# A router's top sixteen taken of two rows in turn, in finer steps between the low parts of streamed weights, and transposes in another ring of PSUM banks

## The chip, the cores and the metric

The kernel runs on one core of one Trainium2 chip. The metric is the device time in microseconds of one execution; the figure to compare is the median of three runs. The program's engines appear in the profile as PE (TensorE matmul) with PEld (its weight loads), DVE (VectorE), ACT (ScalarE), POOL (GpSimd) and SP (SyncE, which issues the DMAs). L12 is line 12 of the kernel.

## What is computed

The reference runs two layers of a first block (a pooling mixer or chunked attention, each followed by a convolutional feed-forward) and one layer of a second block (retention and stick-breaking attention, mixed by gates, followed by a layer of 16384 small experts) on one sequence of 256 positions of width 1024. The change lies in the experts' layer:

```python
def block(xb):
    q = (xb @ w_q).reshape(B, T, PEER_HEADS, 2, PEER_DKEY // 2).astype(jnp.float32)
    s1 = jnp.einsum('bthd,nd->bthn', q[..., 0, :], k1)
    s2 = jnp.einsum('bthd,nd->bthn', q[..., 1, :], k2)
    v1, i1 = lax.top_k(s1, PEER_TOPK)
    v2, i2 = lax.top_k(s2, PEER_TOPK)
    cand_s = (v1[..., :, None] + v2[..., None, :]).reshape(...)
    cand_i = (i1[..., :, None] * N_KEYS + i2[..., None, :]).reshape(...)
    top_s, pos = lax.top_k(cand_s, PEER_TOPK)
    idx = jnp.take_along_axis(cand_i, pos, axis=-1)
    g = jax.nn.softmax(top_s, axis=-1)
    u_sel = jnp.take(u_tab, idx, axis=0)
    h = jnp.einsum('bthkd,btd->bthk', u_sel, xb)
    a = (jax.nn.gelu(h.astype(jnp.float32)) * g).astype(xb.dtype)
    return jnp.einsum('bthk,bthkd->btd', a, jnp.take(v_tab, idx, axis=0))
```

There are 8 heads, 128 keys on either side and 16 kept of each (`PEER_TOPK`), so 128 x 128 experts.

## The kernel before

The kernel doesn't gather the chosen experts. It computes the products of x with all 16384 rows of `peer_u`, multiplies them by gates that are zero for experts not chosen, and multiplies by all rows of `peer_v`. The 256 positions are two blocks of 128. Every product in full precision is made of three matmuls (`mm3`, L107): weights and x are each split into a high part and a low part, the first two matmuls take the weights' high part (L109, L110) and the third their low part (L111).

The weights come from memory as a stream of slabs. For a slab, SP issues a DMA into one of three `raw` buffers, ACT rounds it to the high part `whi` (L72), and DVE (or POOL, for a counted few) subtracts to get the low part `wlo` (L80; L86 where the low parts are put off with `later=True` and given out by `lows`). Three high and three low buffers go round.

The experts' layer is `peer` (L747). PE, DVE and ACT there follow an order written out by hand: each engine runs its instructions in the order in which the program gives them out. Its parts, in time:

1. The query projections, 8 heads, 784.7 to 840.8 us (L777 to L803). For each head h a slab of `peer_wq`, 48 matmuls into the PSUM tile `qps`, and, one head later, `scores` (L968): a copy to SBUF on ACT (L972), 8 matmuls with the keys (`scps`, L976), a scaled copy into a `sc` buffer on ACT (L980). In heads 1 and 2 the normalized x of block 0 and 1 is also transposed (`transposed`, L206): 8 transposes into two PSUM tiles `pt`, read by ACT (L221) and DVE (L223) into `hn`, the x that all experts' products use.
2. The first loop over slabs of `peer_u` (L883), 128 experts and 24 matmuls each, numbered from 0. For slab i the program gives out the high part of slab i + 2 (ACT), some router work (DVE), the low part of slab i + 2 (DVE), and the 24 matmuls of slab i (`up`, PE, into `hps`); every second slab a gelu on ACT (L837). It ends when the router's work has all been given out.
3. The second loop (L905) over the slabs that are left. The 64 groups of four positions get their gates here: one-hot rows on DVE (L859, L862), 8 products on PE (L869, `gps`), and the result multiplied into h on DVE (L877) or copied on ACT (L879). `until` (L903) spreads the 64 groups evenly over the slabs that are left less three. The first products on PE stand behind the second slab of this loop.
4. The products with `peer_v` (L940), 1252 to 1602 us.

How much router work a slab gets is set by `side` (L751). The router is a generator, `route` (L983), that yields a price after each piece. `side(rout, upto)` runs pieces until the sum of the prices reaches `upto`; a yield of 0 (nothing to do yet, or a pause) ends the slab's share and lifts the sum to at least `upto - 1`. `upto` is 5 a head in the projections (L788) and 36 + 1.6 i for slab i (L885).

The router's pieces: for each of 8 heads, 2 blocks and 2 sides, `top16` of a row of 128 scores, price 1.2; then for each block the candidate sums (1.3), `top16` of 8 rows of 64 candidates at 0.9 each, the decoding of the codes `unstair` (L1060, 2.4), and for each side an equality (1.2), a product (1.2) and a tree of sums (L1033 to L1035, 1.4); a softmax with an exponential on ACT, two yields of 0, and three transposes with their copies (1.5). `top16` (L1083) is five VectorE operations: the 8 largest, their places, the row with these struck out, the 8 largest of that, their places. In the trace the searches for places and the striking out appear as two instructions each, a value load and the operation.

PSUM has 8 banks here: the ring "w" has three (`self.nw`), "acc" four, "o" one. In the projections "acc" is used by the score products alone. Of SBUF the router has two scratch rows for `top16` and five `sc` buffers for scores.

Of the kernel before, what the change touches and what calls it, by code (L numbers as in the profile page):

```python
# [8 lines left out]
F32 = mybir.dt.float32  # L9
# [5 lines left out]
OP = mybir.AluOpType  # L15
# [5 lines left out]
KT = D // 128  # L21
# [7 lines left out]
TOPK = 16  # L29
# [5 lines left out]
V_MIX0, V_FFN0, V_MIX1, V_FFN1, V_ATT2, V_FFN2 = 0, 8, 16, 24, 32, 40  # L35
# [11 lines left out]
class K:  # L47
# [155 lines left out]
            nc.scalar.activation(hi, src, AF.Copy, scale=g)  # L203
            nc.vector.scalar_tensor_tensor(lo, src, g, hi.bitcast(F32), op0=OP.mult, op1=OP.subtract)

    def transposed(self, hi, lo, src, b, kts, gcol=None, k0=0):  # L206

        nc = self.nc
        for k in range(0, kts, 4):
            n = min(4, kts - k)  # L210

            tag, bufs = ("o", 1) if kts == KT and b == 1 and k == 4 else ("w", self.nw)
            pt = self.ps.tile([128, 4, 128], F32, tag=tag, name="pt", bufs=bufs)
            for j in range(n):
                nc.tensor.transpose(pt[:, j, :], src[:, (k + j) * 128:(k + j + 1) * 128], self.ident)
            t = slice(b * 128, (b + 1) * 128)
            if gcol is None:
                self.split(hi[:, k0 + k:k0 + k + n, t], lo[:, k0 + k:k0 + k + n, t], pt[:, :n, :])
            else:
                for j in range(n):  # L220
                    nc.scalar.activation(hi[:, k0 + k + j, t], pt[:, j, :], AF.Copy, scale=self.gain(gcol + k + j))  # L221
                for j in range(n):
                    nc.vector.scalar_tensor_tensor(lo[:, k0 + k + j, t], pt[:, j, :], self.gain(gcol + k + j),  # L223
                                                   hi[:, k0 + k + j, t].bitcast(F32), op0=OP.mult, op1=OP.subtract)
# [522 lines left out]
    def peer(self, rt, wq_scope):  # L747
        tc, nc = self.tc, self.nc
# [17 lines left out]
        with ExitStack() as ctx:  # L766
# [6 lines left out]
            rout = self.route(rt["route"], pT, gp, iota)  # L773
            next(rout)
            prev, xn = None, []
            self.to_pool = 7
            for h in range(8):  # L777
                if h == 7:
                    wq = self.next()
                    self.wp = rt["slabs"]  # L780
                    self.nraw, self.nsplit, self.piece = 3, 3, 1024
                    self.start_stream(self.stream2())
                    self.prefetch(2)
                else:
                    self.prefetch(2)
                    wq = self.next()
                wh, wl = wq
                side(rout, h * 5.0)  # L788
                ps = self.ps.tile([128, 2, S], F32, tag="w", name="qps", bufs=self.nw)
                for m in range(2):  # L790
                    for k in range(KT):
                        c = slice(m * 1024 + k * 128, m * 1024 + (k + 1) * 128)
                        self.mm3(ps[:, m], wh[:, c], wl[:, c], self.hT[0][:, k], self.hT[1][:, k],
                                 k == 0, k == KT - 1)
                if prev:
                    self.scores(rt["route"], *prev)
                else:
                    self.r = self.factors()
                    hT = self.ring(rt["hn"], self.OFF)
                    xn = [self.normalized(b) for b in range(2)]  # L800
                if xn and h:
                    self.transposed(*hT, xn.pop(0), h - 1, KT, V_FFN2)
                prev = (h, ps)  # L803
            wq_scope.close()
            self.oh = pool("oh")
# [76 lines left out]
            last = None  # L882
            for i in range(N1):  # L883
                self.prefetch(3, later=True)
                if not side(rout, 36 + i * 1.6):  # L885
                    last = i
                    break
                self.lows()
                up(i)
                if i == 0:  # L890
                    self.scores(rt["route"], *prev)
                if i % 2:
                    gelu(i)
            else:
                last = N1
                for _ in rout:
                    pass
# [22 lines left out]
            acc = self.acc4()  # L920
            AH, AL = self.ring(rt["hn"], 0)
            a = {}
# [45 lines left out]
    def scores(self, rt, h, ps):  # L968

        nc = self.nc  # L970
        q = rt.tile([128, 2, S], F32, tag="pq", name="pq", bufs=2)
        nc.scalar.activation(q, ps, AF.Copy)  # L972
        sp = self.ps.tile([128, 2, 2, 128], F32, tag="acc", name="scps", bufs=4)
        for b in range(2):
            for s in range(2):
                nc.tensor.matmul(sp[:, b, s], q[:, s, b * 128:(b + 1) * 128], self.keys[:, s],  # L976
                                 start=True, stop=True)
        sc = rt.tile([128, 2, 2, 128], F32, tag="sc", name="scores", bufs=5)
        for b in range(2):
            nc.scalar.activation(sc[:, b], sp[:, b], AF.Copy, scale=self.r[b])  # L980
        self.sc.append(sc)

    def route(self, rt, pT, gp, iota):  # L983
# [8 lines left out]
        for h in range(8):  # L992
            while len(self.sc) <= h:
                yield 0
            for b in range(2):
                for s in range(2):
                    self.top16(rt, v[:, b, 2 * h + s], ix[:, b, 2 * h + s], self.sc[h][:, b, s])
                    yield 1.2
        for b in range(2):
            ixf = rt.tile([128, 16, TOPK], F16, tag="ixf", name="ixf", bufs=1)  # L1000
            nc.vector.tensor_copy(ixf, ix[:, b])
# [8 lines left out]
                nc.vector.tensor_tensor(o, v1[:, :, a:a + na, None].to_broadcast([128, 8, na, nb]),  # L1010
                                        v2[:, :, None, 0:nb].to_broadcast([128, 8, na, nb]), op=OP.add)
            yield 1.3
            for h in range(8):
                self.top16(rt, top[:, h], code[:, 2, h], cand[:, h])
                yield 0.9
            abf = rt.tile([128, 2, 8 * TOPK, 2], F16, tag="abf", name="abf", bufs=1)
            self.unstair(rt, abf, code)
            yield 2.4
            sel = rt.tile([128, 3, 8, TOPK], F32, tag="sel", name="sel", bufs=1)
            tt = nc.vector.tensor_tensor  # L1020
            for s in range(2):
                eq = rt.tile([128, 8 * TOPK, TOPK], F16, tag="eq", name="eq", bufs=1)
                of = lambda ap: ap.to_broadcast([128, 8 * TOPK, TOPK // 2, 2])
                tt(eq.rearrange("p k (a b) -> p k a b", b=2),
                   of(iota[:, 0:TOPK].rearrange("p (a b) -> p a b", b=2)[:, None]), of(abf[:, s][:, :, None, :]),
                   op=OP.is_equal)
                yield 1.2
                src = ixf.rearrange("p (h s) a -> p h s a", s=2)[:, :, s]
                e = eq.rearrange("p (h k) a -> p h k a", h=8)
                tt(e, e, src[:, :, None, :].to_broadcast([128, 8, TOPK, TOPK]), op=OP.mult)  # L1030
                yield 1.2

                for n in (8, 4, 2):  # L1033
                    tt(eq[:, :, 0:n], eq[:, :, 0:n], eq[:, :, n:2 * n], op=OP.add)
                tt(sel[:, s].rearrange("p h k -> p (h k)"), eq[:, :, 0], eq[:, :, 1], op=OP.add)  # L1035
                yield 1.4
            g = sel[:, 2]
            nc.vector.tensor_tensor(g, top, top[:, :, 0:1].to_broadcast([128, 8, TOPK]), op=OP.subtract)
            nc.scalar.activation(g, g, AF.Exp)
# [20 lines left out]
    def unstair(self, rt, ab, code):  # L1060

        nc = self.nc
        ts, stt = nc.vector.tensor_scalar, nc.vector.scalar_tensor_tensor
        for n in range(2):
            ts(code[:, n], code[:, 2], 3 - n, None, op0=OP.logical_shift_right)
        c = rt.tile([128, 3, 8, TOPK], F32, tag="codef", name="codef", bufs=1)
        nc.vector.tensor_copy(c, code)
        a, m = c[:, 0], c[:, 1]
        ts(a, a, -1.0, 0.0, op0=OP.add, op1=OP.max)
        stt(a, m, -6.0, a, op0=OP.add, op1=OP.max)  # L1070
        stt(a, c[:, 2], -48.0, a, op0=OP.add, op1=OP.max)
        flat = lambda ap: ap.rearrange("p h k -> p (h k)")[:, :, None].to_broadcast([128, 8 * TOPK, 2])
        nc.vector.tensor_copy(ab[:, 0], flat(a))

        f = rt.tile([128, 8, TOPK], F32, tag="first", name="first", bufs=1)
        ts(f, a, 8.0, 8.0, op0=OP.mult, op1=OP.add)
        stt(f, a, 16.0, f, op0=OP.mult, op1=OP.min)
        ts(m, a, 4.0, 24.0, op0=OP.mult, op1=OP.add)
        nc.vector.tensor_tensor(f, f, m, op=OP.min)
        stt(f, a, 48.0, f, op0=OP.add, op1=OP.min)  # L1080
        nc.vector.tensor_tensor(ab[:, 1], flat(c[:, 2]), flat(f), op=OP.subtract)

    def top16(self, rt, v, ix, s):  # L1083
        nc = self.nc
        t = rt.tile([128, 128], F32, tag="topk", name="topk", bufs=2)[:, :s.shape[1]]
        nc.vector.max(out=v[:, 0:8], in_=s)
        nc.vector.max_index(out=ix[:, 0:8], in_max=v[:, 0:8], in_values=s)  # L1087
        nc.vector.match_replace(out=t, in_to_replace=v[:, 0:8], in_values=s, imm_value=-3.0e38)  # L1088
        nc.vector.max(out=v[:, 8:16], in_=t)
        nc.vector.max_index(out=ix[:, 8:16], in_max=v[:, 8:16], in_values=t)  # L1090

    def finish(self):
        for b in range(2):
# [158 lines left out]
```

## Time and profile before

| | us |
|---|---|
| median of three runs | 1604.07 (1604.07 to 1605.76) |
| the profiled execution | 1604.23 |
| its span, first to last instruction | 1602.5 |
| PE busy / DVE busy / ACT busy / POOL busy in the span | 1565.4 / 1160.3 / 843.0 / 105.0 |

The span holds 26447 instructions, 278.66 MB moved by DMA (174 GB/s in the mean), and a mean granted TensorE clock of 0.995. An instruction's time in a row is from its start to its end; instructions of one engine overlap by a part of that, so what one costs its engine is read from one start to the next. Matmul ends are modelled.

### The profile page before, as it was taken

What the parts mean: (1) busy time and instruction counts of PE and PEld (TensorE: products, weight loads), DVE (VectorE), ACT (ScalarE), POOL (GpSimd) and SP (SyncE); (2) the same over time, 40 slices, a digit from 0 to 9 for tenths busy, and PEclk for the clock granted to TensorE, in tenths of its full rate; (3) what the DMA queues carried; (4) which work ended last, traced back from release to release, by engine and by line L of the source; (5) the groups of instructions that cost most, each with busy time, mean ns of one, the idle gap of its engine ahead of it and who ended that gap; (6) DMA issues with size and microseconds to landing.
All of it is one profiled execution on the core that took longest, in us unless ns stands there. A gap on an engine that the chain in (4) does not pass through costs nothing.

```text
span 1602.5 us, 26447 instructions
## 1 busy us (share of the span) xinstructions
PE 1565.4 (98%) x10190; PEld 1401.5 (87%) x10190; DVE 1160.3 (72%) x2479; ACT 843.0 (53%) x1563; POOL 105.0 (7%) x111
## 2 busy tenths in 40 slices
PE   5999999999999999999999999999999999999999
PEld 4999987779999887888898999999999888888887
DVE  7676777767767877675599987788888655555554
ACT  6555565565555647444554555454444544454453
POOL 5000020010000202000260000000000000000000
PEclk9999999999999999999999999999999999999999
DMA  5555464325555552455424555555555666666664
GB/s 218 181 196 198 168 237 175 132 83 192 201 183 201 187 183 106 152 178 200 167 76 136 167 174 169 170 171 159 170 161 170 186 197 196 189 194 196 194 192 152
DMA packets 58446, 278.66 MB, mean 174 GB/s; under 512 B 6480, under 2 KB 7376, under 8 KB 41680
## 3 DMA queue, kind: packets, MB, share of 16 engines
q1 hardware_dynamic: 58320, 276.97, 52.6%
q8 instruction: 80, 1.31, 0.3%
q14 instruction: 46, 0.38, 0.1%
HBM read 275.90 MB, written 1.05 MB: 173 GB/s over the span
## 4 chain that ended last, share of the span: by engine, by line
PE 87%; DVE 9%; issue 2%; ACT 1%; DMA 1%; POOL 0%; SPq 0%; DVEq 0%; ACTq 0%; POOLq 0%
PE acc L110 15%; PE acc L111 15%; PE acc L109 15%; PE hps L109 6%; PE hps L111 6%; PE hps L110 6%; PE up L110 5%; PE up L111 5%; PE up L109 5%; PE gps L869 2%; DVE wlo L86 1%; DVE wlo L80 1%; DVE topk L1088 1%; DVE ix L1087 1%; DVE ix L1090 1%
## 5 line engine op out<-in xcount | busy, mean ns | idle before, releaser
L72 ACT ACTIVATE whi<-raw 128x512 fp32r<-128x512 f32 (+1 forms) x764 | 556.3, 769 | 381.3 <-PE acc L111 158.4
L80 DVE TENSOR_TENSOR wlo<-raw,whi 128x512 fp32r<-128x512 f32 (+1 forms) x572 | 448.6, 812 | 137.7 <-ACT whi L72 137.5
L111 PE MATMUL hps<-hn,wlo 128*128 128x256 f32 x1024 | 289.2, 282 | 8.6 <-DVE wlo L86 8.5
L109 PE MATMUL hps<-hn,whi 128*128 128x256 f32 x1024 | 293.5, 287 | 0.0
L110 PE MATMUL hps<-hn,whi 128*128 128x256 f32 x1024 | 287.1, 280 | 0.0
L111 PEld LDWEIGHTS hps<-hn,wlo 128*128 128x128 f32 x1024 | 194.0, 189 | 10.7 <-DVE wlo L86 10.6
L110 PE MATMUL up<-hT,whi 128*128 128x256 f32 x704 | 197.8, 281 | 1.5 <-DVE hT L223 1.5
L109 PE MATMUL up<-hT,whi 128*128 128x256 f32 x704 | 198.1, 281 | 0.4 <-DVE hT L223 0.4
L111 PE MATMUL up<-hT,wlo 128*128 128x256 f32 x704 | 197.4, 280 | 0.0
L110 PE MATMUL acc<-wlo,hn 128*128 128x512 f32 x504 | 196.2, 389 | 0.0
L111 PE MATMUL acc<-whi,hn 128*128 128x512 f32 x504 | 196.2, 389 | 0.0
L109 PE MATMUL acc<-whi,hn 128*128 128x512 f32 x504 | 196.2, 389 | 0.0
L110 PEld LDWEIGHTS hps<-hn,whi 128*128 128x128 f32 x1024 | 194.5, 190 | 0.0
L109 PEld LDWEIGHTS hps<-hn,whi 128*128 128x128 f32 x1024 | 194.3, 190 | 0.0
L86 DVE TENSOR_TENSOR wlo<-raw,whi 128x1024 fp32r<-128x1024 f32 x128 | 155.8, 1219 | 14.8 <-ACT whi L72 14.1
L110 PEld LDWEIGHTS up<-hT,whi 128*128 128x128 f32 x704 | 133.6, 190 | 3.3 <-DVE hT L223 2.0
L109 PEld LDWEIGHTS up<-hT,whi 128*128 128x128 f32 x704 | 133.5, 190 | 2.1 <-issue 0.7
L111 PEld LDWEIGHTS up<-hT,wlo 128*128 128x128 f32 x704 | 133.6, 190 | 0.0
L110 PE MATMUL acc<-wlo,hT 128*128 128x512 f32 (+1 forms) x320 | 125.0, 391 | 2.2 <-DVE wlo L80 1.2
L80 POOL TENSOR_TENSOR wlo<-raw,whi 128x512 fp32r<-128x512 f32 x64 | 84.3, 1347 | 636.0 <-ACT whi L72 629.3
L111 PE MATMUL acc<-whi,hT 128*128 128x512 f32 (+1 forms) x320 | 124.7, 390 | 0.0
L109 PE MATMUL acc<-whi,hT 128*128 128x512 f32 (+1 forms) x320 | 124.4, 390 | 0.0
(291 smaller groups left out, 2486.1 us busy)
## 6 DMA issues: line engine op xcount, KB each, us to landing
raw<-in_peer_u SPq DMA_DIRECT2D x128, 512.0 KB, 3.6
raw<-in_peer_v SPq DMA_DIRECT2D x128, 512.0 KB, 3.6
raw<-in_wup SPq DMA_DIRECT2D x44, 1024.0 KB, 4.9
raw<-in_win SPq DMA_DIRECT2D x26, 1024.0 KB, 4.8
raw<-in_wdn SPq DMA_DIRECT2D x22, 1024.0 KB, 4.8
raw<-in_wqkv SPq DMA_DIRECT2D x12, 1024.0 KB, 4.9
raw<-in_wo SPq DMA_DIRECT2D x8, 1024.0 KB, 4.8
raw<-in_peer_wq SPq DMA_DIRECT2D x8, 1024.0 KB, 4.8
```

The source lines that it names most:

```text
L72: i = nc.scalar.activation(hi[:, c:c + n], raw[:, c:c + n], AF.Copy)
L80: low(*args, op=OP.subtract)
L86: self.nc.vector.tensor_tensor(*self.low_parts.pop(0), op=OP.subtract)
L109: mm(ps, lh, rh, start=start, stop=False)
L110: mm(ps, lh, rl, start=False, stop=False)
L111: mm(ps, ll, rh, start=False, stop=stop)
L869: nc.tensor.matmul(ps[:, j], jh[:, j], gh[:, n, j], start=n == 0, stop=n == 1)
L1087: nc.vector.max_index(out=ix[:, 0:8], in_max=v[:, 0:8], in_values=s)
L1088: nc.vector.match_replace(out=t, in_to_replace=v[:, 0:8], in_values=s, imm_value=-3.0e38)
L1090: nc.vector.max_index(out=ix[:, 8:16], in_max=v[:, 8:16], in_values=t)
```

## The change

`top16` takes two rows and gives out each operation for both before the next one, with a price after the first two operations and one after the last three. `unstair` becomes a generator with three prices (1.0, 1.3, 1.4) in place of one of 2.4. A tree of sums is priced 1.9 instead of 1.4. A slab gets 1.5 instead of 1.6. The scratch rows of `top16` have 4 buffers instead of 2, the scores 4 instead of 5. The transposes of the experts' x go into the "acc" ring in place of "w" (and "o" for half of the second block). Apart from the order of the operations, what is computed is the same.

```diff
-    def transposed(self, hi, lo, src, b, kts, gcol=None, k0=0):
+    def transposed(self, hi, lo, src, b, kts, gcol=None, k0=0, bank=None):
...
-            tag, bufs = ("o", 1) if kts == KT and b == 1 and k == 4 else ("w", self.nw)
+            tag, bufs = bank or (("o", 1) if kts == KT and b == 1 and k == 4 else ("w", self.nw))
...
                 if xn and h:
-                    self.transposed(*hT, xn.pop(0), h - 1, KT, V_FFN2)
+                    self.transposed(*hT, xn.pop(0), h - 1, KT, V_FFN2, bank=("acc", 4))
...
-                if not side(rout, 36 + i * 1.6):
+                if not side(rout, 36 + i * 1.5):
...
-        sc = rt.tile([128, 2, 2, 128], F32, tag="sc", name="scores", bufs=5)
+        sc = rt.tile([128, 2, 2, 128], F32, tag="sc", name="scores", bufs=4)
...
             for b in range(2):
-                for s in range(2):
-                    self.top16(rt, v[:, b, 2 * h + s], ix[:, b, 2 * h + s], self.sc[h][:, b, s])
-                    yield 1.2
+                yield from self.top16(rt, 1.2, [(v[:, b, 2 * h + s], ix[:, b, 2 * h + s], self.sc[h][:, b, s])
+                                                for s in range(2)])
...
-            for h in range(8):
-                self.top16(rt, top[:, h], code[:, 2, h], cand[:, h])
-                yield 0.9
+            for h in range(0, 8, 2):
+                yield from self.top16(rt, 0.9, [(top[:, i], code[:, 2, i], cand[:, i]) for i in (h, h + 1)])
             abf = rt.tile([128, 2, 8 * TOPK, 2], F16, tag="abf", name="abf", bufs=1)
-            self.unstair(rt, abf, code)
-            yield 2.4
+            yield from self.unstair(rt, abf, code)
...
-                yield 1.4
+                yield 1.9
...
         ts(a, a, -1.0, 0.0, op0=OP.add, op1=OP.max)
+        yield 1.0
         stt(a, m, -6.0, a, op0=OP.add, op1=OP.max)
         stt(a, c[:, 2], -48.0, a, op0=OP.add, op1=OP.max)
-        flat = lambda ap: ap.rearrange("p h k -> p (h k)")[:, :, None].to_broadcast([128, 8 * TOPK, 2])
         nc.vector.tensor_copy(ab[:, 0], flat(a))
 
         f = rt.tile([128, 8, TOPK], F32, tag="first", name="first", bufs=1)
         ts(f, a, 8.0, 8.0, op0=OP.mult, op1=OP.add)
+        ts(m, a, 4.0, 24.0, op0=OP.mult, op1=OP.add)
+        yield 1.3
         stt(f, a, 16.0, f, op0=OP.mult, op1=OP.min)
-        ts(m, a, 4.0, 24.0, op0=OP.mult, op1=OP.add)
         nc.vector.tensor_tensor(f, f, m, op=OP.min)
         stt(f, a, 48.0, f, op0=OP.add, op1=OP.min)
         nc.vector.tensor_tensor(ab[:, 1], flat(c[:, 2]), flat(f), op=OP.subtract)
-
-    def top16(self, rt, v, ix, s):
-        nc = self.nc
-        t = rt.tile([128, 128], F32, tag="topk", name="topk", bufs=2)[:, :s.shape[1]]
-        nc.vector.max(out=v[:, 0:8], in_=s)
-        nc.vector.max_index(out=ix[:, 0:8], in_max=v[:, 0:8], in_values=s)
-        nc.vector.match_replace(out=t, in_to_replace=v[:, 0:8], in_values=s, imm_value=-3.0e38)
-        nc.vector.max(out=v[:, 8:16], in_=t)
-        nc.vector.max_index(out=ix[:, 8:16], in_max=v[:, 8:16], in_values=t)
+        yield 1.4
+
+    def top16(self, rt, cost, rows):
+
+        vec = self.nc.vector
+        t = [rt.tile([128, 128], F32, tag="topk", name="topk", bufs=4)[:, :s.shape[1]] for _, _, s in rows]
+        for v, _, s in rows:
+            vec.max(out=v[:, 0:8], in_=s)
+        for v, ix, s in rows:
+            vec.max_index(out=ix[:, 0:8], in_max=v[:, 0:8], in_values=s)
+        yield cost
+        for (v, _, s), r in zip(rows, t):
+            vec.match_replace(out=r, in_to_replace=v[:, 0:8], in_values=s, imm_value=-3.0e38)
+        for (v, _, s), r in zip(rows, t):
+            vec.max(out=v[:, 8:16], in_=r)
+        for (v, ix, s), r in zip(rows, t):
+            vec.max_index(out=ix[:, 8:16], in_max=v[:, 8:16], in_values=r)
+        yield cost
```

## Rows read from the trace of the kernel before

**Rows 1.** Stretches: length, busy (instructions) of PE, PEld, DVE, ACT, POOL; PEclk, DMA.

```profile
840.80:952.50 111.70, 103.12 (x833) 101.00 (x832) 102.24 (x325) 55.41 (x68) 0.00 (x0) 0.97 0.51 157
952.50:1252.50 300.00, 300.00 (x2780) 296.91 (x2779) 249.87 (x485) 148.80 (x293) 0.00 (x0) 1.00 0.55 169
```

**Rows 2.** Waits of PE, 784.7 to 952.5: us in total, times, longest.

```profile
PE hps L111 <- DVE wlo L86: 8.5, 9, 2.6
```

**Rows 3.** PE in order of time: start, us, instruction, [idle before <-releaser].

```profile
800.94 0.39 PE L109 MATMUL qps<-hT,whi 128*128 128x256 f32 x1 [2.25 <-DVE hn L223]
...
849.78 0.38 PE L111 MATMUL hps<-hn,wlo 128*128 128x256 f32 x1 [1.98 <-DVE wlo L86]
...
886.26 0.39 PE L111 MATMUL hps<-hn,wlo 128*128 128x256 f32 x1 [1.25 <-DVE wlo L86]
...
928.20 0.39 PE L111 MATMUL hps<-hn,wlo 128*128 128x256 f32 x1 [2.62 <-DVE wlo L86]
```

**Rows 4.** Stretches as in rows 1: two behind long waits, three slabs without one.

```profile
850.73:854.14 3.41, 3.41 (x19) 3.41 (x18) 3.27 (x13) 0.23 (x1) 0.00 (x0) 0.50 0.62 168
929.24:932.65 3.41, 3.41 (x18) 3.41 (x17) 3.38 (x4) 0.00 (x0) 0.00 (x0) 0.50 0.75 259
935.26:943.74 8.48, 8.48 (x75) 8.48 (x74) 7.51 (x10) 5.25 (x6) 0.00 (x0) 1.00 0.69 207
```

**Rows 5.** DVE in order of time: one row of 128 and the next one's start.

```profile
801.83 0.29 DVE L1086 MAX8 v<-scores 128x8 f32<-128x128 f32 x1
802.15 0.09 DVE L1087 MATCH_VALUE_LOAD ix<-v,scores 128x8 f32 x1
802.23 0.28 DVE L1087 FIND_INDEX8 ix<-v,scores 128x8 uint32<-128x128 f32 x1
...
802.49 0.28 DVE L1088 MATCH_REPLACE8 topk<-v,scores 128x128 f32<-128x128 f32 x1
802.80 0.29 DVE L1089 MAX8 v<-topk 128x8 f32<-128x128 f32 x1
803.13 0.09 DVE L1090 MATCH_VALUE_LOAD ix<-v,topk 128x8 f32 x1
803.21 0.28 DVE L1090 FIND_INDEX8 ix<-v,topk 128x8 uint32<-128x128 f32 x1
803.41 0.28 DVE L1086 MAX8 v<-scores 128x8 f32<-128x128 f32 x1
```

**Rows 6.** DVE: a low part, the start of a row of 64, the next low part.

```profile
864.68 1.22 DVE L86 TENSOR_TENSOR wlo<-raw,whi 128x1024 fp32r<-128x1024 f32 x1
865.81 0.22 DVE L1086 MAX8 top<-cand 128x8 f32<-128x64 f32 x1
866.07 0.09 DVE L1087 MATCH_VALUE_LOAD code<-top,cand 128x8 f32 x1
...
867.06 1.21 DVE L86 TENSOR_TENSOR wlo<-raw,whi 128x1024 fp32r<-128x1024 f32 x1
```

**Rows 7.** DVE: decoding, first and last and the low part behind; a tree and what follows.

```profile
890.67 1.65 DVE L1034 TENSOR_TENSOR eq<-eq 128x1024 f16<-128x1024 f16 x3
...
892.82 1.23 DVE L1024 TENSOR_TENSOR eq<-iota,abf 128x2048 f16<-128x2048 f16 x1
...
923.30 0.36 DVE L1065 TENSOR_SCALAR code<-code 128x128 uint32<-128x128 uint32 x2
...
926.92 1.22 DVE L86 TENSOR_TENSOR wlo<-raw,whi 128x1024 fp32r<-128x1024 f32 x1
```

**Rows 8.** Start of the first loop: second head's first row, high parts, slab 2's products, low part.

```profile
811.72 0.28 DVE L1086 MAX8 v<-scores 128x8 f32<-128x128 f32 x1
...
835.34 2.00 ACT L72 ACTIVATE whi<-raw 128x1024 fp32r<-128x1024 f32 x2
...
847.41 0.28 PE L109 MATMUL hps<-hn,whi 128*128 128x256 f32 x1
...
848.52 1.21 DVE L86 TENSOR_TENSOR wlo<-raw,whi 128x1024 fp32r<-128x1024 f32 x1
```

More of the change, by code (lines that the diff above doesn't have):

```diff
@@ L1068, in unstair @@
         a, m = c[:, 0], c[:, 1]
+        flat = lambda ap: ap.rearrange("p h k -> p (h k)")[:, :, None].to_broadcast([128, 8 * TOPK, 2])
         ts(a, a, -1.0, 0.0, op0=OP.add, op1=OP.max)
+        yield 1.0
         stt(a, m, -6.0, a, op0=OP.add, op1=OP.max)
         stt(a, c[:, 2], -48.0, a, op0=OP.add, op1=OP.max)
-        flat = lambda ap: ap.rearrange("p h k -> p (h k)")[:, :, None].to_broadcast([128, 8 * TOPK, 2])
         nc.vector.tensor_copy(ab[:, 0], flat(a))
```

## The prediction

> **What bounds the kernel now.** I read the table by stretches first [rows 1]. In the last stretch of [rows 1], where the experts' up products run beside the gates, PE is busy for all 300.00 us: nothing done on another engine can shorten it. In the stretch before it, 840.80 to 952.50, the up products run beside the router's selection on DVE, and the picture is the reverse: DVE is busy 102.24 of 111.70 us and PE only 103.12, at a granted clock of 0.97. The change works in this stretch and in the query projections just ahead of it, so its worth is read here and not from PE's 98% of the span.
>
> Three losses of PE show there. First, waits: PE stood 8.5 us in nine waits before L111, the first matmul of a slab that needs the slab's low part, and what came last was always DVE's L86 [rows 2]. The largest are 1.98, 1.25 and 2.62 us, and ahead of them one of 2.25 us in the projections, ended by DVE's L223 [rows 3]. Second, the clock: right after the 1.98 and the 2.62 us waits there is a stretch of 3.41 us at 0.50, that is 1.2 instead of 2.4 GHz; the 1.25 us wait has none [rows 4, 3]. At half clock 3.41 us do the work of 1.7 us, so the two cost 3.4 us. Third, waits too short for the view. A slab without a wait takes 8.48 / 3 = 2.83 us [rows 4]. The stretch of 111.70 us holds 34 slabs of 24 matmuls (816 of the 833 counted), 96.1 us, and about 1.2 us of other PE work (eight score products, six transposes). The whole loss is 111.70 - 96.1 - 1.2 = 14.4 us: 8.5 of listed waits, 3.4 of clock, 2.5 of small waits. With the 2.25 us of the projections, 16.6 us is the most that this change can win, unless it touches what the trace doesn't show as lost.
>
> **Why DVE is late.** From slab 0 to the end of the router's work DVE owes, each slab, one low part (1.13 us from start to start) and its share of the selection. A row of 128 takes 803.41 - 801.83 = 1.58 us but is booked at 1.2 [rows 5]; a row of 64 takes 867.06 - 865.81 = 1.25 and is booked at 0.9 [rows 6]; the decoding of the codes (L1065 to L1081) takes 3.62 us and is booked at 2.4, and a reduction tree 2.15 booked at 1.4 [rows 7]. With 1.6 booked units a slab, real work of 12.6 us (8 rows of 128 left) and twice about 25 us (one block's rest: 8 x 1.25 + 3.62 + 2 x 2.15, and some 7 for the pieces booked 7.6 in all), plus 32 low parts (36.2 us), makes 99 us for 32 slabs: 3.09 us a slab against PE's 2.83. Over 32 slabs that is 8.5 us short, the size of the listed waits. The booked sum also gives the 32: 34 are spent when slab 0 begins, 9.6 are left for rows of 128, 20.0 for each block, about 2.5 go in the two empty steps of each block, 86.1 in all, and 36 + 1.6 i reaches that at i = 32.
>
> **The change, part by part.**
> Two rows in turn. In [rows 5] an instruction that needs the result of the one before it starts 0.31 to 0.33 us after it (MAX8 to the value load, replace to MAX8, MAX8 to the value load); one that doesn't starts 0.20 us after it (FIND_INDEX8 at 803.21, next MAX8 at 803.41, though FIND_INDEX8 lasts 0.28). A row has three such places, and with a second row's instruction between, each falls from about 0.315 to 0.20: 0.34 us a row. No row shows a MAX8 followed by an independent instruction; its bounds are 0.20 and 0.32, and I take 0.20, since FIND_INDEX8 reads the same 128 elements and lasts as long. A row of 128 then takes 1.235 us, half a pair 0.97 (two MAX8, two finds) or 1.49 (two replaces, two MAX8, two finds), booked 1.2 each. In a row of 64 the first place is 0.26 [rows 6] and would be about 0.13; three of them make 0.34 as well, so 0.90 a row, booked 0.9. In all 48 x 0.34 = 16 us less on DVE.
>
> The Trainium skill, page "VectorE: DVE Perf Modes", section "The DRAIN you can't avoid", speaks against this: the next VectorE instruction starts only when the pipe is empty, chaining without semaphores doesn't avoid that, so one should save instructions and not waits. By it rows in turn would be no cheaper, which is rival B. The start of MAX8 0.08 us before FIND_INDEX8 ends disagrees, and the section itself exempts instructions that nothing holds.
>
> Finer steps and truer prices. The decoding is booked 1.0 + 1.3 + 1.4 = 3.7 in three steps, a tree 1.9, and a slab gets 1.5. No instruction is added; only the place of the low parts between them moves. Remaining work is 9.9 us (8 rows) and twice about 22.4 (25 less 8 x 0.34), with 37 low parts (41.8): 96.5 us. Booked: 34 + 9.6 + 2 x 22.3 + about 2.3 = 90.5, which 36 + 1.5 i reaches at i = 37. So 2.61 us a slab against 2.83: DVE gains 0.2 a slab and stays ahead. The longest block between two low parts falls from 4.9 us (a row of 64 and the decoding) to about 3.
>
> The start is the tight place, so I follow it. All of PE and ACT comes 2.25 us earlier (next paragraph). The two high parts on ACT begin at 835.34 [rows 8], so at 833.1, the first ends 1.05 later, 834.1; DVE then does two low parts (2.3), the sixth head (4 x 1.235), half a head (2.46) and the low part of slab 2 (1.13 + 0.08): 845.0. Slab 2 began at 847.41 [rows 8], so at 845.2, and its third matmul needs the low part at 845.4: 0.4 us to spare, where before DVE only began it at 848.52. For slab 4 (steps 0.97; 1.49 + 0.97; with two low parts) it is done at about 850.7 and wanted at 851.1, 0.4 us; for slab 5, 0.7; for slab 6, 1.4. I leave 0.4 us for small waits there; the ends are 0 and 2.
>
> Transposes in the "acc" banks. Before, the first block's two transposes hold two of the three "w" banks while the projection before them holds the third, so head 2's projection waits until L223 has read one: the 2.25 us [rows 3]. With four "acc" banks, of which a head's scores take one, the projection finds a "w" bank free and starts behind the last transpose. Gain 2.25 us; POOL's low part for that slab is done by then. For the second block no wait shows, and I take nothing; bounds 0 and 2.25 for the part as a whole. The score products now share the ring with them; each ring place was read a whole head (6 us and more) earlier.
>
> Four score buffers for five. ACT's copy of head 7's scores now waits for the selection of head 3, and behind it on ACT would queue slab 3's high part and the gelus. Head 3 is done three heads of 4.94 us after 809.5 (811.72 - 2.25), near 825 if its scores don't come later; the copy stands behind slab 0's products, which begin at 840.8 - 2.25 and take 2.83, past 841: cost nothing. Were DVE 16 us late there, PE would wait for what exceeds that. The fourth selection buffer only removes reuse.
>
> What is late next. In the third stretch the 64 groups of gates spread over 125 - 37 = 88 slabs instead of 93. DVE is busy 249.87 of 300 us there [rows 1]; of that 94 low parts are 106 at 1.13 each, the rest, 144, grows by 93/88, 8 us: 258 of 300. PE still sets the pace, so this costs nothing.
>
> **Sum.** 14.4 + 2.25 - 0.4 = 16.2 us. The profiled execution took 1604.23 us (span 1602.5), 0.16 over the median of the runs: 1604.23 - 16.2 = 1588.0 us. With the small losses above, about 0.7 of doubt in the pace of a clean slab over 34 slabs, and 1 us between builds, this case spans 1586.0 to 1590.2.
>
> **The rivals.**
> B, rows in turn are no cheaper (1.57 and 1.24 us as before). DVE was without a gap from 811.72 [rows 8]; from 809.5 on, 22 rows (34.5) and three low parts (3.4) end at 847.4, 2.0 us after slab 2 wants it; such a wait brought a clock fall, 1.7. Then 3.09 us a slab over five slabs loses 1.2, and the rows of 64 (1.5 / 0.9 x 1.24 + 1.13 = 3.2 a slab) about 1.8 in either block. Some 8.3 of the 16.6 stay: 1604.2 - 8.3 = 1595.9. For it speaks that no row shows one MAX8 behind another; against it the 0.20 us behind FIND_INDEX8.
> C, the start is late: 0.4 us is little, and 1 to 2 us lost at slabs 2 to 4 keep the first clock fall: 1588.0 + 1.3 + 1.7 = 1591.0.
> D, the banks bring nothing, because the transposes now wait in the "acc" ring or the projection for something else just behind: 1590.3.
> E, slower than before: in the third stretch, from slab 37, a slab lasts 300 / 94 = 3.19 us, and DVE's part of it is 2.66 and would be 2.74. If the denser placing made it need over 3.43, the 16.2 won would be lost again in 88 slabs, and at 3.5 the time would be 1588.0 + 88 x 0.31 = 1615. DVE lies 0.7 a slab below that point.
>
> **Chances.** Forecast 0.78, B 0.07, C 0.09, D 0.03, E 0.02, no change (the won time is lost to waits that I don't see) 0.01. A difference of under 0.2% (3.2 us) can't be told from none. Range: the forecast's own, carried up over C and D to 1592.5, holds about 0.85 by these chances; B lies outside. Faster 0.97, same 0.01, slower 0.02.
>
> **What the next profile would show.** Right: no wait of PE for L86 over 0.5 us and none for L223 at head 2, both stretches at 0.50 gone, pairs of MAX8 0.20 us apart, first gate product behind slab 38, DVE below 98% from slab 6 on, third stretch still all PE. Wrong: MAX8 to MAX8 at 0.3 (B); a wait of a microsecond at slab 2 or 4 with a half-clock stretch behind it (C); PE's wait at head 2 with another name (D); PE waiting for L862 or L86 after slab 40 (E).

## The result

| | before | after |
|---|---|---|
| median | 1604.07 us | 1587.76 us |
| all runs | 1603.95 to 1605.76 | 1586.78 to 1588.03 |
| ratio, with 95% interval | | 0.9894 [0.9882, 0.9907] |
| the profiled execution / its span | 1604.23 / 1602.5 us | 1586.78 / 1585.1 us |
| its mean granted clock | 0.995 | 0.998 |

The kernel became 16.3 us faster, against 16.2 forecast (1588.0). Run once more beside three of the experiments, the changed kernel took 1586.65 us, a ratio of 0.9889 [0.9873, 0.9906].

The first view of after is again the table by stretches, in the columns of [rows 1] (the last number is GB/s). The first row is the stretch from slab 0 of the first loop on, the second lies wholly in the second loop.

```profile
838.50:952.50 114.00, 114.00 (x984) 113.96 (x982) 103.44 (x332) 63.42 (x79) 0.00 (x0) 1.00 0.60 181
...
960.00:1230.00 270.00, 270.00 (x2524) 267.38 (x2523) 229.81 (x456) 132.01 (x265) 0.00 (x0) 1.00 0.55 166
```

Against [rows 1], PE was busy for 103.12 of 111.70 us and now is for all of 114.00, at full clock. DVE went from 92% to 91% busy: it does less for the router, but in the same time more low parts and already some gates. What it lost is lateness, not work to do. The second loop is still PE's; DVE has 85% there against 83% in [rows 1].

The view of PE's waits from 780 to 950 us (total, times, longest) lists these two and no others; the waits of [rows 2] and the 2.25 us of [rows 3] are gone:

```profile
PE qps L110 <- DVE hT L223: 0.5, 1, 0.5
PE pt L215 <- DVE x L240: 0.3, 1, 0.3
```

Both stand at the start of the first projection, where nothing was changed. At head 2's projection, where [rows 3] show 2.25 us, the matmuls of `qps` now follow the transposes at once (PE in order of time: start, us, line, instruction):

```profile
797.66 1.04 PE L215 MATMUL pt<-ident,hn 128*128 128x128 f32 x8
798.46 0.37 PE L109 MATMUL qps<-hT,whi 128*128 128x256 f32 x1
```

And this is a pair of rows on DVE, to be laid beside [rows 5]. The two operations of one kind are merged into one line where they follow each other:

```profile
801.85 0.48 DVE L1088 MAX8 v<-scores 128x8 f32<-128x128 f32 x2
802.24 0.07 DVE L1090 MATCH_VALUE_LOAD ix<-v,scores 128x8 f32 x1
802.30 0.29 DVE L1090 FIND_INDEX8 ix<-v,scores 128x8 uint32<-128x128 f32 x1
...
803.28 0.48 DVE L1095 MAX8 v<-topk 128x8 f32<-128x128 f32 x2
803.67 0.07 DVE L1097 MATCH_VALUE_LOAD ix<-v,topk 128x8 f32 x1
...
804.19 0.47 DVE L1088 MAX8 v<-scores 128x8 f32<-128x128 f32 x2
```

From the first MAX8 to the value load behind both are 802.24 - 801.85 = 0.39 us, so 0.195 for each MAX8. The pair takes 804.19 - 801.85 = 2.34 us, 1.17 a row against 1.58 in [rows 5].

The tight place at the start of the first loop came out a little better than followed by hand. The low part of slab 2 starts at 843.28 and the matmul that needs it at 845.20 (DVE and PE, in order of time; slab 2's first matmul is the L109 here):

```profile
843.28 1.21 DVE L86 TENSOR_TENSOR wlo<-raw,whi 128x1024 fp32r<-128x1024 f32 x1
```

```profile
844.97 0.28 PE L109 MATMUL hps<-hn,whi 128*128 128x256 f32 x1
...
845.20 0.28 PE L111 MATMUL hps<-hn,wlo 128*128 128x256 f32 x1
```

It ends at 844.49, 0.71 us early, where 0.4 was forecast; in [rows 8] it only began at 848.52. The first product of the gates on PE follows the last matmul of slab 38:

```profile
949.23 0.62 PE L869 MATMUL gps<-gh,hot 128*128 128x128 f16 x8
```

### The profile page after: what moved, and what is told of

It is laid out like the page before. It is cut to its first block, busy times and chain, and to the rows that moved or that the text cites. A ratio compares the mean times of both kernels' runs of the same rounds, so it can differ in the third digit from the quotient of the medians.

```text
span 1585.1 us, 26448 instructions
## 1 busy us (share of the span) xinstructions
PE 1559.0 (98%) x10190; PEld 1397.6 (88%) x10190; DVE 1145.6 (72%) x2478; ACT 841.9 (53%) x1559; POOL 105.1 (7%) x111
## 4 chain that ended last, share of the span: by engine, by line
PE 93%; DVE 2%; issue 1%; POOL 1%; ACT 1%; DMA 1%; SPq 0%; POOLq 0%; ACTq 0%; DVEq 0%
PE acc L111 15%; PE acc L110 15%; PE acc L109 15%; PE hps L109 8%; PE hps L111 8%; PE hps L110 8%; PE up L110 5%; PE up L111 5%; PE up L109 5%; PE gps L869 2%; POOL wlo L80 1%; PE qps L110 1%; PE qps L109 1%; PE qps L111 1%; PE pt L215 1%
## 5 line engine op out<-in xcount | busy, mean ns | idle before, releaser
L109 PE MATMUL hps<-hn,whi 128*128 128x256 f32 x1024 | 291.8, 285 | 0.0
L109 PE MATMUL up<-hT,whi 128*128 128x256 f32 x704 | 198.1, 281 | 0.5 <-ACT hT L221 0.5
L109 PE MATMUL acc<-whi,hn 128*128 128x512 f32 x504 | 196.1, 389 | 0.0
L109 PEld LDWEIGHTS hps<-hn,whi 128*128 128x128 f32 x1024 | 192.7, 188 | 0.0
L109 PEld LDWEIGHTS up<-hT,whi 128*128 128x128 f32 x704 | 133.5, 190 | 2.1 <-ACT hT L221 0.7
L109 PE MATMUL acc<-whi,hT 128*128 128x512 f32 (+1 forms) x320 | 124.5, 391 | 0.0
```

The source lines that it names most:

```text
L109: mm(ps, lh, rh, start=start, stop=False)
```

## Experiments

Two theories are kept apart. By the first, that of the prediction's sum, the parts add: each removes a loss of its own. By the second, what counts is only how early DVE is at each low part; then parts can stand in for each other, and a gain ahead of a late DVE is given back.

### One part alone, or one part less

**The banks alone**, in the kernel before:

```diff
-                    self.transposed(*hT, xn.pop(0), h - 1, KT, V_FFN2)
+                    self.transposed(*hT, xn.pop(0), h - 1, KT, V_FFN2, bank=("acc", 4))
```

> The kernel before with one part of the change: the transposes of the experts' x in the "acc" ring. Theory P (the parts add): the wait of 2.25 us at head 2's projection goes and nothing else changes, 1604.1 - 2.25 = 1601.8 us. Theory L (what counts is how late DVE is): PE comes 2.25 us earlier to slab 2, but DVE, which runs without a gap from 811.72 on and stood only 1.45 us before the second block's L223, can come at most 1.45 us earlier; the wait before slab 2's low part grows from 1.98 to about 2.8 us, and the gain is about 1.4 us: 1602.7. Rival D (the wait moves to the "acc" ring): no gain, 1604.1.

Measured: 1600.8 us against 1603.99 for the kernel before on that chip, ratio 0.9984 [0.9974, 0.9993]. The time alone would speak for the adding theory (3.2 us won, 2.25 forecast); the trace doesn't. PE's wait at head 2 is gone, but these are its waits for low parts now, in order of time, to be laid beside [rows 3]:

```profile
847.80 0.39 PE L111 MATMUL hps<-hn,wlo 128*128 128x256 f32 x1 [2.89 <-DVE wlo L86]
...
854.78 0.38 PE L111 MATMUL hps<-hn,wlo 128*128 128x256 f32 x1 [1.11 <-DVE wlo L86]
...
863.97 0.39 PE L111 MATMUL hps<-hn,wlo 128*128 128x256 f32 x1 [0.52 <-DVE wlo L86]
...
926.37 0.39 PE L111 MATMUL hps<-hn,wlo 128*128 128x256 f32 x1 [2.63 <-DVE wlo L86]
```

```profile
PE hps L111 <- DVE wlo L86: 10.8, 10, 2.9
```

The total is 10.8 us; before it was 8.5 for low parts and 2.25 at head 2, 10.75 in all [rows 2, 3]. Total waits mislead here, because the clock differs too: this trace has no stretch at half clock in the first loop, where [rows 4] have two. What DVE did settles it. These two low parts are the ones of [rows 8] (848.52) and [rows 6] (864.68):

```profile
846.54 1.21 DVE L86 TENSOR_TENSOR wlo<-raw,whi 128x1024 fp32r<-128x1024 f32 x1
...
862.70 1.22 DVE L86 TENSOR_TENSOR wlo<-raw,whi 128x1024 fp32r<-128x1024 f32 x1
```

Both are 1.98 us earlier than before, 0.43 of it because this execution was that much ahead at the first projection already (784.28 against 784.71). So the wait at slab 2 grew by 0.91 us, to 2.89 (2.8 expected), and the last long wait ends 1.83 us earlier (926.37 against 928.20), 1.4 without the 0.43: the second theory's gain. The other 1.7 of the 3.5 us between the two spans come behind that wait, where before has its second half-clock stretch [rows 4]: the first gate product, at 948.98 against 952.50, is 3.52 us earlier. The first half-clock stretch cost nothing. The two low parts are 16.16 us apart with it as without it, so DVE set the pace there, and without it PE waits at slabs 4 and 7 instead (1.11 and 0.52 us). The executions of this kernel lay between 1599.39 and 1604.46 us; the two over 1604 had mean clocks of 0.994 and 0.993, the others 0.995 to 0.998.

**All but the banks**: the changed kernel with the diff above undone.

> The changed kernel without the banks: the transposes of the experts' x go into "w" (and "o") again. Prediction's term: the wait of 2.25 us on L223 at head 2's projection is back, and nothing else changes, since DVE then has that much more time ahead of slab 2: 1587.8 + 2.25 = 1590.0 us. Rival (the gain is given back further on, as in the kernel with the banks alone): 1588.5 to 1589.

Measured: 1589.73 us, ratio 0.9911 [0.9894, 0.9927]. The trace has the wait on L223 again and none in the first loop.

```profile
800.88 0.38 PE L109 MATMUL qps<-hT,whi 128*128 128x256 f32 x1 [2.25 <-DVE hn L223]
```

From slab 0's first matmul to the last one of the second loop this trace has 394.25 us, and so has the changed kernel's. So the banks are worth their whole 2.25 us only where DVE isn't late behind them; in the kernel before, the same edit won about 1.4 by its trace.

**Rows one after the other**, with all else as changed:

```diff
-        for v, _, s in rows:
-            vec.max(out=v[:, 0:8], in_=s)
-        for v, ix, s in rows:
+        for v, ix, s in rows:
+            vec.max(out=v[:, 0:8], in_=s)
             vec.max_index(out=ix[:, 0:8], in_max=v[:, 0:8], in_values=s)
...
-        for (v, _, s), r in zip(rows, t):
-            vec.match_replace(out=r, in_to_replace=v[:, 0:8], in_values=s, imm_value=-3.0e38)
-        for (v, _, s), r in zip(rows, t):
-            vec.max(out=v[:, 8:16], in_=r)
         for (v, ix, s), r in zip(rows, t):
+            vec.match_replace(out=r, in_to_replace=v[:, 0:8], in_values=s, imm_value=-3.0e38)
+            vec.max(out=v[:, 8:16], in_=r)
             vec.max_index(out=ix[:, 8:16], in_max=v[:, 8:16], in_values=r)
```

> The changed kernel with the rows of a pair one after the other inside each step (steps, prices, budget and banks as changed). My theory: a row of 128 takes 1.57 us again and one of 64 1.24, DVE is late at slab 2 by 2 to 3.4 us with a fall of the clock behind it, and waits of up to 1 us come back at slabs 4, 10, 11 and 29: 7 to 9.5 us lost, 1595 to 1597. Rival: the finer steps and the new prices are what counts, rows in turn are an extra: 1588 to 1590.

Measured: 1595.07 us, ratio 0.9941 [0.9925, 0.9958], as this theory said and outside its rival. Four of the five waits in the trace (5.1 us in all) stand at slabs where they were expected, 2, 4, 10 and 11; the fifth is at slab 27 instead of 29. The first two:

```profile
848.40 0.39 PE L111 MATMUL hps<-hn,wlo 128*128 128x256 f32 x1 [2.93 <-DVE wlo L86]
...
854.98 0.38 PE L111 MATMUL hps<-hn,wlo 128*128 128x256 f32 x1 [0.71 <-DVE wlo L86]
```

The second half of a row shows the dependence again: MAX8 starts 0.31 us behind the replace, the value load 0.34 behind MAX8.

```profile
803.21 0.28 DVE L1092 MATCH_REPLACE8 topk<-v,scores 128x128 f32<-128x128 f32 x1
803.52 0.30 DVE L1093 MAX8 v<-topk 128x8 f32<-128x128 f32 x1
803.86 0.09 DVE L1094 MATCH_VALUE_LOAD ix<-v,topk 128x8 f32 x1
```

One part of the expectation missed: no fall of the clock came behind the 2.93 us.

**The old steps**: rows in turn and banks as changed, but a pair, and the decoding, in one step each at the old prices, and 1.6 a slab.

```diff
-        yield cost
         for (v, _, s), r in zip(rows, t):
             vec.match_replace(out=r, in_to_replace=v[:, 0:8], in_values=s, imm_value=-3.0e38)
...
-        yield cost
+        yield 2 * cost
...
-        yield 1.0
...
-        yield 1.3
...
-        yield 1.4
+        yield 2.4
...
-                yield 1.9
+                yield 1.4
...
-                if not side(rout, 36 + i * 1.5):
+                if not side(rout, 36 + i * 1.6):
```

> The changed kernel with the old steps: a pair of rows, and the whole decoding, are one step each, at the old prices (2.4, 1.8, 2.4, 1.4) and 1.6 a slab; rows in turn and banks as changed. My theory: with 16 us less on DVE the slabs' shares fit, 2.8 us a slab; what the coarse steps cost is a wait of about 0.7 us at slab 4 and one of about 0.7 behind the second decoding, no fall of the clock: 1587.8 + 1.4 = 1589.2. Rival (steps and prices carry the gain): the waits behind the decodings of 1.25 and 2.62 us stay, with a fall of the clock, 1587.8 + 5.6 = 1593.4.

Measured: 1588.61 us, ratio 0.9902 [0.9886, 0.9919]; PE waits 0.41 us at slab 4 and 0.82 behind the second decoding, and nowhere else. Once rows in turn have made the work cheaper, steps and prices are worth 1 to 2 us together.

**Rows one after the other, priced at what they take:**

```diff
-                yield from self.top16(rt, 1.2, [...
+                yield from self.top16(rt, 1.57, [...
...
-                yield from self.top16(rt, 0.9, [...
+                yield from self.top16(rt, 1.24, [...
```

> As the kernel with the rows of a pair one after the other, but half a pair is priced at what it takes, 1.57 for rows of 128 and 1.24 for rows of 64 (instead of 1.2 and 0.9), with 1.5 a slab. Theory P (rows in turn are needed): as that kernel, 1595 to 1597. Theory L (DVE only has to be early at each low part): a slab gets 1.5 us of real work and a low part, 2.63 us against 2.80; less selection is given out ahead of slab 0, so slab 2 is in time too; the router's work ends some ten slabs later (about slab 48) and the gates go into 77 slabs instead of 88, where DVE has room: no wait, 1587.8.

Measured: 1587.25 us, ratio 0.9897 [0.9881, 0.9914], with no wait of PE for a low part. Its row for the stretch of the first table is as full as the changed kernel's:

```profile
838.50:952.50 114.00, 114.00 (x980) 114.00 (x979) 103.21 (x336) 59.51 (x72) 0.00 (x0) 1.00 0.58 184
```

So rows in turn aren't needed for the gain. Two prices win back the 8 us that this order of the rows lost under the old ones.

**Five numbers alone**, in the kernel before:

```diff
-                if not side(rout, 36 + i * 1.6):
+                if not side(rout, 36 + i * 1.5):
...
-                    yield 1.2
+                    yield 1.57
...
-                yield 0.9
+                yield 1.24
...
-            yield 2.4
+            yield 3.6
...
-                yield 1.4
+                yield 2.1
```

> The kernel before with five numbers changed and nothing else: a row of 128 priced 1.57, a row of 64 1.24, the decoding 3.6, a tree 2.1, and 1.5 a slab. No rows in turn, no finer steps, no banks. Theory L (DVE only has to be early at each low part): the wait of 2.25 us at head 2 stays, the others go, 1590.0 us with the first gate products about slab 50. Rival (rows in turn and finer steps are needed, so that the low part is late behind the whole decoding): waits of 1 us or more behind the two decodings, 1592 to 1594.

Measured: 1590.79 us against 1604.74 on that chip, ratio 0.9914 [0.9897, 0.9930]. PE's waits from 780 us to the end of the second loop, ahead of the two of the changed kernel's list and behind them:

```profile
PE qps L109 <- DVE hn L223: 2.3, 1, 2.3
...
PE hps L111 <- DVE wlo L86: 0.3, 1, 0.3
```

That is 14 of the 18 us that the changed kernel won on the same chip (1586.65). Where the rest lies can be read from the two traces, whose spans are 4.5 us apart: 1.5 us ahead of the first projection, where the kernels are the same (785.49 against 784.00), 2.5 in the projections, which is the banks, and 0.5 behind. From slab 0's first matmul to the last one of the second loop it is 409.28 us before, 394.71 here and 394.25 in the changed kernel: in the two loops five numbers win 14.6 of 15.0 us, without rows in turn, finer steps or other buffers.

### The share of a slab, more and less

Each of these is the changed kernel with one number in `side(rout, 36 + i * 1.5)` changed.

**2.0:**

> The changed kernel with 2.0 instead of 1.5 of router work a slab. Prediction's account: DVE owes 2.0 + 1.13 = 3.1 us a slab against PE's 2.80, the work ends near slab 29, and PE waits about 6 us in waits of up to 1 us: 1587.8 + 6.1 = 1593.9, by a fall of the clock 1.7 us more. Rival (the share per slab hardly matters once rows go in turn and steps are fine): 1588 to 1589.

Measured: 1593.69 us, ratio 0.9933 [0.9916, 0.9949], with seven listed waits for low parts, 3.4 us in all:

```profile
PE hps L111 <- DVE wlo L86: 3.4, 7, 0.9
```

The view lists no more of the 6 us lost. The account by prices holds on the other side of PE's pace too.

**0.75:**

> The changed kernel with 0.75 instead of 1.5 of router work a slab. The router's work then ends near slab 70 and the 64 groups of gates share some 55 slabs, 1.16 a slab. Prediction's account: a group costs DVE about 1.53 us, so a slab needs 1.13 + 1.16 x 1.53 = 2.9 us of DVE and 2.83 + 1.16 x 0.43 = 3.3 of PE: PE still sets the pace, 1587.8 us, at most 2 us more where two groups fall into one slab. Rival E (the denser second loop makes DVE or the chain place, product, one-hot the bound): 0.3 us or more a slab over 55 slabs, 1604 or more.

Measured: 1595.82 us, ratio 0.9950 [0.9934, 0.9967]: 8 us lost, neither the account's 0 to 2 nor the rival's 16, but by the rival's mechanism. Two stretches of this kernel, the first loop and the second, in the columns of the first table:

```profile
840.00:1035.00 195.00, 195.00 (x1674) 195.00 (x1673) 134.01 (x339) 99.01 (x117) 0.00 (x0) 1.00 0.62 184
1050.00:1230.00 180.00, 177.00 (x1678) 170.79 (x1677) 177.74 (x405) 79.03 (x176) 0.00 (x0) 1.00 0.47 148
```

In the second DVE is busy 177.74 of 180 us. Its operations there, by line (count, busy us, mean ns):

```profile
L86 DVE TENSOR_TENSOR wlo<-raw,whi 128x1024 fp32r<-128x1024 f32 x50 | 60.9, 1218 | 0.0
...
L859 DVE TENSOR_TENSOR hot<-iota,pT 128x1024 f16<-128x1024 f16 x58 | 39.7, 685 | 0.2 <-PE gps L869 0.2
```

180 us less 50 low parts at 1.13 leave 123.5 for 58 groups, 2.13 us a group. My 1.53 had counted the one-hots and left out a part of the placing and the gelu's multiplications. With 2.13, DVE takes over at one group a slab (1.13 + 2.13 = 3.26 against 2.83 + 0.43 for PE).

**1.0**, to test that corrected account:

> The changed kernel with 1.0 instead of 1.5 a slab; the router's work ends near slab 54 and the 64 groups share 71 slabs, 0.90 a slab. The kernel at 0.75 showed 2.13 us of DVE a group beside a low part of 1.13 a slab; so a slab needs 1.13 + 0.90 x 2.13 = 3.05 of DVE and 2.83 + 0.90 x 0.43 = 3.22 of PE. Account: PE still sets the pace, 1587.8 us (up to 1 more); DVE would take over at one group a slab, near slab 61. Rival (the loss grows in proportion from 1.5 to 0.75): 1590.5.

Measured: 1586.91 us, beside 1586.65 for the changed kernel on the same chip, with no wait. Its DVE is busy 243.68 of 270 us in the second loop, and PE all of it:

```profile
960.00:1230.00 270.00, 270.00 (x2536) 267.26 (x2535) 243.68 (x491) 134.68 (x261) 0.00 (x0) 1.00 0.53 165
```

So the time is flat from 1.0 to 1.5 and rises on either side, at 2.0 in the first loop and at 0.75 in the second.

### A delay put in by hand, and the clock

In the changed kernel slab 14's low part, which was 2.81 us early, is computed k times more ahead of itself:

```diff
+                if i == 12:
+                    for _ in range(k):
+                        nc.vector.tensor_tensor(*self.low_parts[0], op=OP.subtract)
                 self.lows()
```

**k = 3:**

> The changed kernel with slab 14's low part computed four times (three times 1.25 us added). PE should wait 3.75 - 2.81 = 0.9 us at slab 14 and about 0.5 soon after. No fall of the clock (before, a wait of 1.25 us had none): 1587.8 + 1.4 = 1589.2, mean clock as in the changed kernel. If a fall comes behind such a wait too: 1590.9 and a mean clock lower by 0.001.

Measured: 1588.39 us, ratio 0.9899 [0.9882, 0.9915], 1.7 over the changed kernel beside it; waits of 0.87 and 0.49 us, no fall of the clock behind them.

**k = 5:**

> The changed kernel with slab 14's low part computed six times over on DVE (five times 1.25 us added at one place). It was 2.81 us early, so PE should wait 6.25 - 2.81 = 3.4 us at slab 14 and about 0.6 soon after. Theory W (a wait of 2 us or more brings a stretch of 3.41 us at half clock): 1587.8 + 4.0 + 1.7 = 1593.5, in every execution. Theory V (whether the clock falls behind such a wait differs from one execution to the next): 1591.8 in some and 1593.5 in others, and the mean granted clock differs with it by 0.001.

Measured: 1593.88 us (1592.02 to 1594.72), ratio 0.9936 [0.9919, 0.9952]; with a mean clock of 0.996 in all four executions. That mean alone doesn't tell where the clock fell: the changed kernel has 0.997 or 0.998 in the first comparison and 0.996 to 0.998 in the second, where its trace has a fall at 19 us, in a part of the program that no edit here touches. The wait, and a stretch at half clock from its last half microsecond on:

```profile
882.60 0.58 PE L111 MATMUL hps<-hn,wlo 128*128 128x256 f32 x1 [3.39 <-DVE wlo L86]
```

```profile
882.14:885.55 3.41, 2.95 (x14) 2.95 (x15) 3.31 (x7) 0.00 (x0) 0.00 (x0) 0.50 0.48 149
```

Theory W fits this trace. It doesn't fit the others: the 6 us behind the wait of 2.93 us (rows one after the other) and those behind the 2.63 us (the banks alone) ran at full clock,

```profile
848.40:854.40 6.00, 5.87 (x48) 5.67 (x48) 5.72 (x24) 1.38 (x2) 0.00 (x0) 1.00 0.54 175
```

```profile
926.37:932.00 5.63, 5.63 (x48) 5.63 (x49) 5.56 (x6) 0.66 (x1) 0.00 (x0) 1.00 0.59 193
```

while before, a wait of 1.98 us was followed by a fall [rows 3, 4]. What decides, besides the wait, is open, and so is the spread of 2.7 us between this kernel's executions, of which the profiled one is the shortest.

**The changed kernel again**, on the chip and beside the runs of the five numbers, of 1.0 a slab and of k = 3:

> The changed kernel once more, beside the other three on one chip: 1587.8 us, with no wait of PE for a low part of the first loop.

Measured: 1586.65 us, with the same two short waits ahead of the projections and no other.

## Why the prediction was right, and where its steps were not

**The loss and its place.** Right. The 16.6 us read as lost in [rows 1 to 4] are the gain: profiled spans 17.4 us apart, medians 16.3. All listed waits went, at every slab, and so did both half-clock stretches. A clean slab takes 2.80 us rather than 2.83, which is most of the 1 us by which the spans moved more than the sum; several slabs of the trace of before take 2.80 already, so the loss was read about 1 us too small.

**Why DVE was late.** Right, and the experiments make it the whole story: real work sold too cheaply. The booking argument (32 and 37 slabs) came out to the slab: the first gate product stands behind slab 38, as forecast. The kernel with five numbers changed shows that correct prices are enough for the first loop: 14.6 of the 15.0 us by which the two loops became shorter. So it was the second theory that held: what counts is how early DVE is at each low part.

**Two rows in turn.** The mechanism is right, the size was a little low: 0.41 us a row instead of 0.34. Of the 0.07 about 0.04 are two searches a row that start sooner behind their value load (0.06 us, 0.08 in [rows 5]). MAX8 behind MAX8 takes 0.195, the lower bound. The Trainium skill, page "VectorE: DVE Perf Modes", section "Rules for kernel authors", advises for chained VectorE operations to keep their number low and not the semaphores. Here the same instructions in another order took 1.17 instead of 1.58 us a row, so for this chain the measurement decides against that advice.

**Rival B.** Its time was right (1595.9 forecast, 1595.07 measured), its make-up not: it counted 1.7 us for a fall of the clock that didn't come in that trace, and had the rest too small by 0.7 (6.6 us of waits forecast, 7.3 us between the medians), so that the time came out within 1 us in part by luck. Its own terms add up to 8.5, too, where it writes 8.3. It also held only under the changed prices. The step of the prediction that failed is to take rows in turn as the condition for the gain: with rows one after the other and true prices the time is the changed kernel's.

**The banks.** The sum was right for the whole change (1589.73 without them, 2 us more) and would have been wrong for the banks alone, which win about 1.4 us there because DVE is late behind them.

**The parts I put at nothing.** Four score buffers cost nothing: ACT has no wait on DVE for the scores in the trace of after. The denser second loop cost nothing at 88 slabs or at 71. It does decide near 55 slabs, which is rival E with a price that I had set too low per group in the experiment on 0.75, though not in the prediction, which took DVE's busy time as a whole. The point at which the prediction would lose the gain again, 3.43 us a slab, is 3.37 by its own numbers (3.19 + 16.2 / 88); DVE's part of a slab stayed clear of either.

**The clock.** The prediction said that a wait of 2.0 us "brought a clock fall". That is what [rows 3, 4] show, but as a rule it fell: waits of 2.93, 2.89 and 2.63 us had none. Nor did the two falls cost 3.4 us beside the waits: the one behind slab 2 stood where DVE set the pace, and without it (the banks alone) PE waits instead.

## What to carry to other kernels

Where side work is dealt out beside a bound engine by prices, compare each piece's price with its start-to-start time in the trace before anything is reordered: five numbers alone won 14 of the 18 us here. Follow the deadline of each shared step (here the low part, two slabs ahead) by hand through the tightest place, because a gain ahead of a late engine is given back there. Small dependent VectorE instructions can be put in turn with an independent chain, which here took 0.11 to 0.14 us off each place that waited; it shortens the kernel only where VectorE sets the pace.

## What was not expected of the hardware

The clock didn't fall behind waits of PE of 2.93, 2.89 and 2.63 us, and did behind 1.98, 2.62 and 3.39. Two executions of one and the same kernel (the banks alone) differ by up to 5 us, the longest with the lowest mean clocks. A comparison in which PE waits for a few microseconds at a time therefore needs the clock of each execution beside its time; of the 14.4 us that were read as lost in the trace of before, one fall's 1.7 belong to it, and the other fall's 1.7 stand where DVE was late anyway.
